# First norm's shift and scale as rows by TensorE, directly behind x's transposes, with the mLSTM constants made between products

## The chip, the cores and the metric

The kernel runs on one core of a Trainium2 chip. The metric is device time in microseconds: the median of three timed runs of the kernel before is 1879.92 us (1876.63 to 1886.28). One further execution was recorded by the hardware profiler.

## The reference, cut to what matters

The program is one layer of a hybrid block: a modulated norm, a projection, an mLSTM mixer beside dilated attention, and an expert-choice feed-forward part. The change touches the first step and a few constants.

```python
mod = silu(c) @ w_ada + b_ada                 # c: 1 x 1024, w_ada: 1024 x 6144
shift1, scale1, gate1, shift2, scale2, gate2 = split(mod, 6)
h = rms_norm(x, norm1_g) * (1 + scale1) + shift1   # x: 1024 x 1024
proj = h @ w_in                                    # 1024 x 2576
```

Of the mLSTM only this matters here: q and k come from the same 4x4 block-diagonal maps, so the kernel forms, for each of four heads, one 128x128 matrix amat (q's map times k's map) and bdv (v's map) from w_q_blk, w_k_blk and w_v_blk.

## The kernel before, in words

`phase_start` does all of the first stage. x comes as eight tiles of 128 tokens (0.52 MB each) by SP's DMA queue. ACT squares each and sums it up (L216), DVE forms the reciprocal roots by a Newton iteration of eleven small operations for four tiles at a time (L134 to L139) and scales the tiles (L244). PE transposes them in two groups of 32 (g = 0 and 1, L248), and ACT and DVE copy the results into xT, which holds k, the 128-wide pieces of the model dimension, in the partitions (L250, L252).

Shift and scale of the norm must stand in the partitions too, one column for each k. `ada_load(k)` fetches w_ada's columns of one k in four DMAs with runs of 512 bytes (L205). For k = 0, PE multiplies them with silu(c) in 16 one-column products (L235). For the others DVE sums eight pieces, each scaled by silu(c) (`ada_sum`, L319 and L321), and PE adds up the partitions by a product with ones (L269). `modulate(k)` then adds the bias and the norm's gain on DVE (L272, L273), POOL applies shift and scale to xT (L274), and `split` makes hTh (fp32r, ACT, L124) and the rest hTl (DVE, L125).

The products of this stage (`mm3_stat`, L332, L334, L336) take three of the four 128-wide chunks of the first 512 columns of w_in, for k = 0 to 7: wh hTh, wh hTl and wl hTh, each for two halves of the tokens, 18 products of 128x512 for a k. The fourth chunk follows for all k, 48 products. So there are 192 products, and behind them the gate projection `gates_proj` begins with the tile wg_h (L332 again). Weights are fetched, copied and split by `w_pair` (L345 on ACT, L346 on DVE or POOL); attention's tables make three small products (L675).

Ahead of it, `consts` has ACT issue ten small DMAs: w_q_blk, w_k_blk and w_v_blk (L155) and seven vectors into the rows of vrows (L170), which PE transposes into vcols (L178, `consts2`). `mlstm_consts` makes masks on POOL, block-diagonal tiles bd on DVE (L442), transposes them on PE (L446, copied at L448), and multiplies them (L451). Both stand in the program between the squares and the roots.

Each engine takes its instructions in the order of the program, apart from small shifts that the build makes; PSUM tiles come from two pools of four (pa and pb), so an order can also wait for a buffer.

Of the kernel before, what the change touches and what calls it, by code (L numbers as in the profile page):

```python
# [16 lines left out]
OP = mybir.AluOpType  # L17
# [93 lines left out]
class K:  # L111
# [30 lines left out]
    def consts(self):  # L142
# [10 lines left out]
        for q, name in enumerate(("w_q_blk", "w_k_blk", "w_v_blk")):  # L153
            src = I[name]
            nc.scalar.dma_start(out=self.w4[:, q], in_=bass.AP(tensor=src.tensor, offset=src.offset, ap=[[4, P], [4 * P, MH], [1, 4]]))  # L155
# [12 lines left out]
        for name, n in (("b_ada", 48), ("norm1_g", 8), ("conv_w", 20), ("conv_b", 4), ("mlstm_norm_g", 4), ("mlstm_skip", 4), ("norm2_g", 8)):  # L168
            src = I[name]
            nc.scalar.dma_start(out=rows[at:at + n, :], in_=bass.AP(tensor=src.tensor, offset=src.offset, ap=[[P, n], [1, P]]))  # L170
# [15 lines left out]
    def phase_start(self):  # L186
# [5 lines left out]
        wada = I["w_ada"].rearrange("(p k) (j n) -> p k j n", k=KT, j=6)  # L192
        with ExitStack() as st:
# [4 lines left out]
            aws, his, los = [], [], []  # L198

            def ada_load(k):  # L200
                aw = [xp.tile([P, KT // 2, 2, P], F32, name="ada_w", **(dict(tag="x", bufs=NT) if 2 <= k < 6 else dict(bufs=4)))
                      for _ in range(2)]
                for h, t in enumerate(aw):
                    for j in range(2):
                        nc.sync.dma_start(out=t[:, :, j, :], in_=wada[:, h * KT // 2:(h + 1) * KT // 2, j, P * k:P * (k + 1)])  # L205
                aws.append(aw)
# [4 lines left out]
            ada_load(0)  # L211
            ada_load(1)
# [5 lines left out]
            self.mlstm_consts()  # L218
            self.consts2()
            accs, pcs = [], []  # L220

            def w_next():
                hi, lo = self.w_pair(0, 512, len(his) // 2, nc.gpsimd if len(his) // 2 % 2 else nc.vector)
                his.extend(hi)
                los.extend(lo)

            def ada_acc(k):

                pcs.append(None)
                if k == 0:  # L230
                    accs.append(None)
                    pcs[k] = self.psB.tile([P, 512], F32, name="pb")
                    for j in range(2):
                        for q in range(KT):
                            nc.tensor.matmul(pcs[k][:, j:j + 1], aws[k][q // 4][:, q % 4, j, :], self.sc[:, q:q + 1], start=(q == 0), stop=(q == KT - 1))  # L235
                else:
# [4 lines left out]
            for g in range(2):  # L241
# [14 lines left out]
                else:  # L256
                    ada_acc(1)
                    for k in range(2, KT):
                        ada_load(k)
# [1462 lines left out]
```

## Time and profile before

| | us |
|---|---|
| median of three timed runs | 1879.92 |
| profiled execution, its own time | 1884.02 |
| its span in the trace | 1882.3 |
| first product of the stage starts | 41.68 |
| first product of the gate projection starts | 100.19 |

Times in a timeline count from the span's start. A matmul's end is modelled, so a row's length has a tail beyond the start of the next one; the pace of a run is read from the starts. An fp32 product shows as two matmul records (two passes), a transpose or an fp32r product as one. Granted clock is the share of TensorE's full speed, 1.00 or 0.50.

### The profile page before, as it was taken

The numbers are of one execution on the slowest core, as the hardware profiler recorded it, in microseconds if no ns is written. First come the engines' busy times: TensorE is split into PE (matmuls) and PEld (weight loads), VectorE is DVE, ScalarE is ACT, GpSimd is POOL, SyncE is SP. The second block draws the span as 40 slices with busy tenths as digits, with TensorE's granted clock in tenths as the row PEclk, the third lists the DMA queues.
The fourth block names the chain that finished last, engine by engine and source line by source line (L and its number), as shares of the span: only waits on it lengthen the run. The fifth ranks groups of instructions, "written<-read, shape, count | busy, mean of one in ns | idle before, by whom it ended". The sixth has DMA issues, their size and how long they took to land. (4 is left out here: it accounts for less than half of the span.)

```text
span 1882.3 us, 23755 instructions
## 1 busy us (share of the span) xinstructions
PE 1774.4 (94%) x8457; PEld 1380.5 (73%) x8457; DVE 1406.9 (75%) x2146; ACT 1119.4 (59%) x1549; POOL 182.6 (10%) x176
## 2 busy tenths in 40 slices
PE   6899999989998939999999999999999999999997
PEld 5677888778886827777777777777777777777775
DVE  5868885687865777777777887777876777867765
ACT  4346454367763537576676666655765766666554
POOL 1301000031123010000100100100100001000000
PEclk9999999999998959999999999999999999999999
DMA  7444663324557777999999999999999989999991
GB/s 234 112 124 141 212 215 110 103 80 117 136 126 210 270 297 291 350 361 356 381 345 367 385 340 368 354 350 359 354 348 351 370 339 376 343 347 344 333 364 34
DMA packets 164492, 517.36 MB, mean 275 GB/s; under 512 B 34614, under 2 KB 68790, under 8 KB 126742
## 3 DMA queue, kind: packets, MB, share of 16 engines
q1 hardware_dynamic: 149376, 482.07, 69.9%
q0 software_dynamic: 10208, 33.10, 7.0%
q8 instruction: 66, 1.08, 0.2%
q10 hardware_dynamic: 4790, 0.68, 0.2%
q14 instruction: 52, 0.43, 0.1%
HBM read 488.29 MB, written 27.50 MB: 274 GB/s over the span
## 5 line engine op out<-in xcount | busy, mean ns | idle before, releaser
L1482 DVE TENSOR_TENSOR wl<-w,wh 128x2048 fp32r<-128x2048 f32 x260 | 585.3, 2280 | 93.1 <-ACT wh L1481 92.5
L1481 ACT ACTIVATE wh<-w 128x2048 fp32r<-128x2048 f32 x260 | 492.3, 1913 | 180.9 <-PE py L1502 80.7
L1481 ACT ACTIVATE wh<-w_half 128x1024 fp32r<-128x1024 f32 x152 | 154.1, 1058 | 68.9 <-PE py L1502 34.9
L1482 DVE TENSOR_TENSOR wl<-w_half,wh 128x1024 fp32r<-128x1024 f32 x152 | 179.0, 1221 | 12.0 <-ACT wh L1481 11.8
L1502 PE MATMUL px<-wh,xTh 128*128 128x512 f32 x448 | 131.4, 411 | 2.1 <-ACT xTh L124 1.6
L1502 PE MATMUL py<-wh,xTh 128*128 128x512 f32 x448 | 131.3, 410 | 1.4 <-ACT wh L1481 1.2
L1502 PE MATMUL py<-wl,xTh 128*128 128x512 f32 x448 | 125.7, 400 | 5.6 <-DVE wl L1482 5.4
L1502 PE MATMUL px<-wl,xTh 128*128 128x512 f32 x448 | 126.3, 402 | 4.4 <-DVE wl L1482 4.4
L1502 PE MATMUL px<-wh,xTl 128*128 128x512 f32 x448 | 124.0, 397 | 0.0
L1502 PE MATMUL py<-wh,xTl 128*128 128x512 f32 x448 | 123.4, 395 | 0.0
L1502 PE MATMUL px<-wh,hT 128*128 128x512 f32 x448 | 118.1, 405 | 0.0
L1502 PE MATMUL py<-wh,hT 128*128 128x512 f32 x448 | 118.1, 405 | 0.0
L1561 POOL DMA_INDIRECT out_dram<-xin,idx x16 | 43.4, 2710 | 673.9 <-DVE xin L1560 673.9
L1502 PEld LDWEIGHTS px<-wl,xTh 128*128 128x128 f32 x448 | 83.6, 189 | 29.3 <-DVE wl L1482 9.5
L1502 PEld LDWEIGHTS py<-wl,xTh 128*128 128x128 f32 x448 | 82.6, 188 | 30.0 <-DVE wl L1482 11.2
L1502 PEld LDWEIGHTS px<-wh,xTh 128*128 128x128 f32 x448 | 83.3, 190 | 28.1 <-issue 6.7
L1502 PEld LDWEIGHTS py<-wh,xTh 128*128 128x128 f32 x448 | 82.9, 188 | 27.1 <-issue 7.7
L1502 PEld LDWEIGHTS px<-wh,hT 128*128 128x128 f32 x448 | 83.2, 188 | 22.8 <-issue 3.8
L1502 PEld LDWEIGHTS py<-wh,hT 128*128 128x128 f32 x448 | 83.0, 188 | 22.8 <-issue 3.8
L1502 PEld LDWEIGHTS px<-wh,xTl 128*128 128x128 f32 x448 | 84.8, 189 | 19.3
L1502 PEld LDWEIGHTS py<-wh,xTl 128*128 128x128 f32 x448 | 84.1, 188 | 19.2 <-DVE xTl L125 0.2
L388 PE MATMUL pa<-wh,hTh 128*128 128x512 f32 x192 | 80.1, 418 | 1.3 <-ACT wh L345 1.2
(458 smaller groups left out, 3371.0 us busy)
## 6 DMA issues: line engine op xcount, KB each, us to landing
w<-in_w_gate_dram SPq DMA_DIRECT2D x100, 1024.0 KB
w<-in_w_up_dram SPq DMA_DIRECT2D x96, 1024.0 KB
w<-in_w_down_dram SPq DMA_DIRECT2D x96, 1024.0 KB
w_half<-in_w_down_dram SPq DMA_DIRECT2D x62, 512.0 KB
w_half<-in_w_up_dram SPq DMA_DIRECT2D x58, 512.0 KB
w_half<-in_w_gate_dram SPq DMA_DIRECT2D x54, 512.0 KB
ada_w<-in_w_ada_dram SPq DMA_DIRECT2D x96, 256.0 KB
wraw<-in_w_in_dram SPq DMA_DIRECT2D x20, 512.0 KB
```

Of the source, the lines that this page charges most:

```text
L388: nc.tensor.matmul(ps, hTh[:, k, t], hi[k], start=(k == 0), stop=False)
L1481: self.nc.scalar.activation(h[:, c], t, AF.Copy)
L1482: self.tc.keep_in_program_order(self.nc.vector.tensor_sub(l[:, c], t, h[:, c]))
L1502: nc.tensor.matmul(ps[c], x[:, t], y[o // m][:, o % m:o % m + 512], start=first and q == 0 and t == 0, stop=last and (q, t) == (len(prods) ...
L1561: nc.gpsimd.indirect_dma_start(out=self.out, out_offset=bass.IndirectOffsetOnAxis(ap=u["idx"][:, :1], axis=0), in_=y, in_offset=None, comp ...
```

## The change

Shift and scale are made for four k at a time (`ada_half(b)`). silu(c) is repeated into 32 columns (screp). For one row of 512 values (shift or scale of four k) PE runs eight products of 32x512, whose outputs stand in four groups of 32 partitions side by side, two products adding up in each. ACT (shift) or DVE (scale) copies the result into SBUF, and four one-column products with sel, which picks one partition of each of the four groups, add the groups up and turn the row into columns. w_ada is fetched in runs of 2048 bytes. `modulate` runs on DVE. Half 0 stands behind all 64 transposes, half 1 behind the products of k = 1. `mlstm_consts` becomes a generator that is advanced between the products of the k's; its masks and `consts2` come after the transposes in the program. All weight splits are on DVE, and the first two weight tiles are fetched earlier. The ten small DMAs are issued by POOL instead of ACT.

```diff
@@ consts @@
-            nc.scalar.dma_start(out=self.w4[:, q], in_=...)
+            nc.gpsimd.dma_start(out=self.w4[:, q], in_=...)
...
-            nc.scalar.dma_start(out=rows[at:at + n, :], in_=...)
+            nc.gpsimd.dma_start(out=rows[at:at + n, :], in_=...)
@@ phase_start @@
+            def ada_load(n, ts):
+                ada[n] = [t.rearrange("p (a n) -> p a n", a=2) for t in ts]
+                for q, t in enumerate(ada[n]):
+                    nc.sync.dma_start(out=t, in_=wada[:, 2 * q:2 * q + 2, n * 512:(n + 1) * 512])
...
-            ada_load(0)
-            ada_load(1)
+            was_x = lambda: [xp.tile([P, D], F32, name="ada_w2", tag="x", bufs=NT) for q in range(4)]
+            own = lambda: [xp.tile([P, D], F32, name="ada_w", bufs=4) for q in range(4)]
+            ada_load(0, own())
+            raws[0] = self.w_raw(0, 512, 0)
...
-            self.mlstm_consts()
-            self.consts2()
+            screp = xp.tile([P, KT, 32], F32, name="silu_c32")
+            nc.vector.tensor_copy(screp, self.sc[:, :, None].to_broadcast([P, KT, 32]))
+            sel = xp.tile([P, 1], F32, name="sel")
+            nc.vector.tensor_reduce(sel, self.ident[:, 0:P:32], axis=AX.X, op=OP.add)
...
                 if g == 0:
-                    ada_acc(0)
-                    w_next()
-                else:
-                    ada_acc(1)
-                    for k in range(2, KT):
-                        ada_load(k)
+                    ada_load(2, was_x())
+                    raws[1] = self.w_raw(0, 512, 1)
+            self.consts2()
+            w_next()
+            consts = self.mlstm_consts()
+            next(consts)
+            def ada_half(b):
+                pc = self.psB.tile([P, 2, 4], F32, name="pb")
+                for j in range(2):
+                    ws = ada[2 * j + b]
+                    ps = self.psB.tile([P, 512], F32, name="pb")
+                    for k in range(KT):
+                        g = slice(32 * (k % 4), 32 * (k % 4) + 32)
+                        nc.tensor.matmul(ps[g, :], screp[:, k, :], ws[k // 2][:, k % 2, :], start=(k < 4), stop=(k >= 4))
+                    row = ws[0][:, 0, :]
+                    if j:
+                        nc.vector.tensor_copy(row, ps)
+                    else:
+                        nc.scalar.activation(row, ps, AF.Copy)
+                    for q in range(4):
+                        nc.tensor.matmul(pc[:, j, q:q + 1], row[:, q * P:(q + 1) * P], sel, start=True, stop=True)
+                mod = xp.tile([P, 2, 4], F32, name="mod", bufs=2)
...
+            def modulate(k):
+                mod = mods[k // 4]
+                nc.vector.tensor_scalar(xT[:, k, :], xT[:, k, :], mod[:, 1, k % 4:k % 4 + 1], mod[:, 0, k % 4:k % 4 + 1], op0=OP.mult, op1=OP.add)
+                self.split(self.hTh[:, k, :], self.hTl[:, k, :], xT[:, k, :])
+            side = itertools.chain(consts, self.attn_tables())
+            ada_half(0)
+            ada_load(1, own())
+            ada_load(3, was_x())
+            for k in range(2):
+                modulate(k)
+            w_next()
+            pss = [[self.xps(t) for b in range(2)] for t in range(3)]
             for k in range(KT):
+                if k % 2 == 0 and k >= 2 and k + 2 < KT:
                     w_next()
                 for c in range(3):
                     self.mm3_stat(pss[c], his[k][:, c * P:(c + 1) * P], los[k][:, c * P:(c + 1) * P], k)
-                if k >= 2:
-                    next(tables, 0)
+                if k == 1:
+                    ada_half(1)
+                if k + 2 < KT:
+                    modulate(k + 2)
+                next(side, 0)
+                if k >= 4:
+                    next(side, 0)
@@ mlstm_consts @@
         for h in range(MH):
+            yield
```

The first place is PE from its start to the first products (L332 before, L338 now; vrows the vector rows, bd and bdT mLSTM constants). Before:

```order
L178 MATMUL pa<-ident,vrows 128x128
L446 MATMUL pb<-ident,bd 128x128 x2
L451 MATMUL pb<-bdT_177,bdT_171 128x128
...
L248 MATMUL pb<-ident,x 128x128 x32
L235 MATMUL pb<-silu_c,ada_w 128x1 x16
L248 MATMUL pb<-ident,x 128x128 x32
L269 MATMUL pb<-ones,ada_acc 128x1 x2
L332 MATMUL pa<-hTh,wh 128x512 x4
```

Now, on the same engine and stretch:

```order
L235 MATMUL pb<-ident,x 128x128 x16
L178 MATMUL pa<-ident,vrows 128x128
L235 MATMUL pb<-ident,x 128x128 x48
L257 MATMUL pb<-ada_w,silu_c_149 32x512 x8
L264 MATMUL pb<-sel,ada_w 128x1 x4
L257 MATMUL pb<-ada_w_219,silu_c_149 32x512 x2
...
L264 MATMUL pb<-sel,ada_w_219 128x1 x4
L338 MATMUL pa<-hTh,wh 128x512 x4
```

The transposes come first, the transpose of vrows stands after 16 of them, and two rows with their column products stand ahead of the first product of the stage.

The second place is PE between the products of the first k's. Before, behind most of the products of k = 1:

```order
L332 MATMUL pb<-hTh,wh 128x512 x2
L334 MATMUL pb<-hTl,wh 128x512
L269 MATMUL pb<-ones,ada_acc 128x1 x2
L334 MATMUL pb<-hTl,wh 128x512
L336 MATMUL pb<-hTh,wl 128x512 x2
L269 MATMUL pb<-ones,ada_acc 128x1 x2
```

Now, at the same place and a little on:

```order
L342 MATMUL pb<-hTh,wl 128x512 x2
L257 MATMUL pb<-ada_w,silu_c_149 32x512 x8
L338 MATMUL pa<-hTh,wh 128x512 x2
L340 MATMUL pa<-hTl,wh 128x512 x2
L264 MATMUL pb<-sel,ada_w 128x1 x4
L257 MATMUL pb<-ada_w_359,silu_c_149 32x512 x2
```

Half 1 took the place of the pairs of L269, of which there was one for each k. Four products of k = 2 stand between its first row and that row's column products.

The third place is POOL's start: ident is the identity that all transposes use, bmask the mask of the mLSTM constants. Before:

```order
masks.py:197 MEMSET ident 128x128
L422 MEMSET mask 128x256
masks.py:199 ISA
masks.py:199 AFFINE_SELECT ident<-ident 128x128
L423 AFFINE_SELECT mask<-mask 128x128
```

Now:

```order
masks.py:197 MEMSET ident 128x128
L155 DMA w_80<-in_w_q_blk_dram 128x4x4
masks.py:199 ISA
masks.py:199 AFFINE_SELECT ident<-ident 128x128
L155 DMA w_80<-in_w_k_blk_dram 128x4x4
L155 DMA w_80<-in_w_v_blk_dram 128x4x4
L170 DMA vrows<-in_b_ada_dram 48x128
```

The ten DMAs, of which six more rows follow here, stand ahead of every mask, one of them between the two steps that make ident.

## Rows read from the trace of the kernel before

**Rows 1.** The page, first part: busy time and share of the span, PE first.
```profile
PE 1774.4 (94%) x8457; PEld 1380.5 (73%) x8457; DVE 1406.9 (75%) x2146; ACT 1119.4 (59%) x1549; POOL 182.6 (10%) x176
```

**Rows 2.** Stretches: length, each engine's busy us, clock, DMA share, GB/s.
```profile
0.00:9.00 9.00, 0.00 (x0) 0.00 (x0) 0.30 (x2) 1.26 (x1) 2.69 (x13) 1.00 0.81 230
...
9.00:16.00 7.00, 2.47 (x8) 1.48 (x8) 3.04 (x15) 6.99 (x15) 0.00 (x0) 1.00 1.00 354
...
16.00:26.00 10.00, 7.01 (x24) 4.77 (x25) 7.80 (x35) 3.74 (x10) 0.00 (x0) 1.00 1.04 287
...
32.60:39.30 6.70, 6.70 (x33) 6.70 (x33) 4.56 (x10) 2.30 (x4) 1.20 (x1) 0.50 0.79 230
...
41.68:100.19 58.51, 52.20 (x222) 38.46 (x223) 46.87 (x96) 18.75 (x20) 19.14 (x20) 1.00 0.47 129
```

**Rows 3.** Waits until 100 us: waiter <- releaser: total us, times, longest.
```profile
ACT hTh L124 <- POOL xT L274: 19.6, 6, 6.8
...
ACT L213 <- DMA vrows<-in_conv_w_dram: 7.7, 1, 7.7
...
PE pa L332 <- ACT hTh L124: 4.8, 4, 1.9
...
PE pa L334 <- DVE hTl L125: 2.6, 4, 1.2
```

**Rows 4.** Timeline to 42 us: start, length, engine, line, operation, count, idle before.
```profile
9.14 1.04 ACT L216 ACTIVATE xT<-x 128x1024 f32<-128x1024 f32 x1
...
20.98 2.74 DVE L244 TENSOR_SCALAR x<-x,rs 128x1024 f32<-128x1024 f32 x4
...
23.64 0.16 DVE L134 TENSOR_SCALAR n_v<-ss 128x4 f32<-128x4 f32 x1
...
23.78 5.98 PE L248 MATMUL pb<-ident,x 128*128 128x128 f32 x29 [0.19 <-DVE x L244]
...
25.82 2.74 DVE L244 TENSOR_SCALAR x<-x,rs 128x1024 f32<-128x1024 f32 x4
...
33.59 6.51 PE L248 MATMUL pb<-ident,x 128*128 128x128 f32 x32
...
40.58 1.05 ACT L124 ACTIVATE hTh<-xT 128x1024 fp32r<-128x1024 f32 x1
...
41.68 1.20 PE L332 MATMUL pa<-hTh,wh 128*128 128x512 f32 x4 [1.24 <-ACT hTh L124]
```

**Rows 5.** Timeline of PE where the gate projection begins.
```profile
99.74 0.61 PE L336 MATMUL pb<-hTh,wl 128*128 128x512 f32 x2
100.19 0.62 PE L332 MATMUL pa<-hTh,wg_h 128*128 128x512 f32 x2
```

**Rows 6.** Timeline, prices of single kinds: ACT copy, column products, small DVE, fp32 passes.
```profile
24.36 0.60 ACT L252 ACTIVATE xT<-pb 128x512 f32<-128x512 f32 x1 [3.50 <-DMA mk<-in_c_mask_dram]
...
29.60 4.13 PE L235 MATMUL pb<-silu_c,ada_w 128*128 128x1 f32 x32
...
51.38 0.23 DVE L272 TENSOR_TENSOR mod<-pb,vcols 128x1 f32<-128x1 f32 x2 [0.36 <-PE pb L269]
...
157.40 1.98 PE L543 MATMUL pb<-xc,amat 128*128 128x512 f32 x4
...
159.22 0.60 PE L553 MATMUL pb<-ident,xc 128*128 128x128 f32 x4
...
159.65 1.06 PE L561 MATMUL pb<-bdv,xm 128*128 128x128 f32 x8
...
441.57 1.09 PE L863 MATMUL op<-pT,vs 128*64 128x128 f32 x16
```

**Rows 7.** Groups until 100 us: busy, mean ns: the second half of a split.
```profile
L125 DVE TENSOR_TENSOR hTl<-xT,hTh 128x1024 fp32r<-128x1024 f32 x8 | 9.7, 1218 | 3.3 <-ACT hTh L124 3.2
```

**Rows 8.** Timeline of POOL: a DMA that it issues itself.
```profile
143.22 0.77 POOL L509 DMA_DIRECT2D gate_rows_d<-row_W  x1 [1.62 <-ACT row_W L505]
```

**Rows 9.** Line 1561: durations in ns, least, median and most.
```profile
L1561 POOL DMA_INDIRECT out_dram<-xin,idx x16: 1552/3381/3402, 822.6 to 1872.0; - x16
```

More of the change, by code (lines that the diff above doesn't have):

```diff
@@ L169, in consts @@
             src = I[name]
-            nc.scalar.dma_start(out=rows[at:at + n, :], in_=bass.AP(tensor=src.tensor, offset=src.offset, ap=[[P, n], [1, P]]))
+            nc.gpsimd.dma_start(out=rows[at:at + n, :], in_=bass.AP(tensor=src.tensor, offset=src.offset, ap=[[P, n], [1, P]]))
             self.vec_rows[name] = at
@@ L253, in phase_start @@
                 if g == 0:
-                    ada_acc(0)
-                    w_next()
-                else:
-                    ada_acc(1)
-                    for k in range(2, KT):
-                        ada_load(k)
-            tables = self.attn_tables()
-            pss = None
-            def modulate(k):
-                pc = pcs[k]
-                if pc is None:
-                    pc = self.psB.tile([P, 512], F32, name="pb")
-                    for j in range(2):
-                        nc.tensor.matmul(pc[:, j:j + 1], accs[k][:, j, :], self.ones[:, 0:1], start=True, stop=True)
-                mod = xp.tile([P, 2], F32, name="mod", bufs=2)
-                for j in range(2):
-                    nc.vector.tensor_add(mod[:, j:j + 1], pc[:, j:j + 1], self.vcol("b_ada", 8 * j + k))
-                nc.vector.scalar_tensor_tensor(mod[:, 1:2], mod[:, 1:2], 1.0, self.vcol("norm1_g", k), op0=OP.add, op1=OP.mult)
-                nc.gpsimd.tensor_scalar(xT[:, k, :], xT[:, k, :], mod[:, 1:2], mod[:, 0:1], op0=OP.mult, op1=OP.add)
-                self.split(self.hTh[:, k, :], self.hTl[:, k, :], xT[:, k, :])
@@ L277, in phase_start @@
-            modulate(0)
-            for k in range(KT):
-                if k and k + 1 < KT:
-                    ada_acc(k + 1)
-                if k + 1 < KT:
-                    modulate(k + 1)
-                if k % 2 == 0 and k + 2 < KT:
-                    w_next()
-                if pss is None:
-                    pss = [[self.xps(t) for b in range(2)] for t in range(3)]
+                    ada_load(2, was_x())
+                    raws[1] = self.w_raw(0, 512, 1)
+            self.consts2()
@@ new lines, in phase_start @@
+            w_next()
+            consts = self.mlstm_consts()
+            next(consts)
+            mods = []
+            def ada_half(b):
[14 more added lines that the diff above has]
+                mod = xp.tile([P, 2, 4], F32, name="mod", bufs=2)
+                for j in range(2):
+                    nc.vector.tensor_add(mod[:, j], pc[:, j], self.vcol("b_ada", 8 * j + 4 * b, 4))
+                nc.vector.scalar_tensor_tensor(mod[:, 1], mod[:, 1], 1.0, self.vcol("norm1_g", 4 * b, 4), op0=OP.add, op1=OP.mult)
+                mods.append(mod)
@@ L292, in phase_start @@
+            for _ in side:
                 pass
```

48 lines of the change are left out of this document (17 added, 31 removed).

## The prediction

> **What bounds the kernel now.** I read the page's first part, then the table of stretches, the list of waits of the first 100 us, and the timelines of PE, DVE, ACT and POOL there. Over the whole execution PE is busy 94% [rows 1], and from the gate projection (its first product at 100.19 us, [rows 5]) on, the order of instructions is the same in both kernels on all five engines. So what the change does to the time is what it does to that moment; everything later should move with it. The profiled execution took 1884.02 us (span 1882.3); the median of the three timed runs is 1879.92. I work out a difference from the profiled execution and apply it to the median.
>
> The 100.19 us have two parts. Until 41.68 us PE waits for the front: x must land, be squared, scaled and transposed, and one k be modulated [rows 4]. Between 41.68 and 100.19 PE is the bound with holes: 192 products at 0.226 us (two start 0.45 us apart, [rows 5]) are 43.4 us of 58.5 [rows 2]; 7.4 us are waits for hTh and hTl [rows 3], and hTh in turn waited 19.6 us for POOL's modulation; the rest are three table products, six pairs of column products of L269 and shorter holes.
>
> **The front, part by part.** (1) *ACT's queue.* Ten DMA issues leave ACT, whose first activation waited 7.7 us behind them [rows 3]. ACT then squares each x as it lands. Until 9 us 230 GB/s arrive, 2.07 MB, about four tiles of 0.52 MB; until 16 us another 354 GB/s [rows 2], which carries the eighth to some 15.3 us. The fourth is squared (1.04 us and the accumulator's read, [rows 4]) at 10.4.
> (2) *DVE.* Before, the reciprocal roots stood among the mLSTM constants and the first x was scaled at 20.98 [rows 4]. Now the eleven small operations come at once (23.64 to 25.82, 2.2 us, [rows 4]) and four scalings of 0.69 (2.74 for four): all four x's at 15.3. The second four: squared at 16.7; six mask products moved ahead of the roots cost 1.5 us inside this gap (estimate: 0.25 each, an eighth of the 1.22 of 128x1024 with two inputs, [rows 7], and 0.1); roots 2.2, the copy of vcols 0.3 (an estimate like the 0.25), scaling 2.7: 22.0 to 23, I take 22.
> (3) *Transposes.* 32 of them took 6.51 us at a granted clock of 0.50 ([rows 2], [rows 4]); four elsewhere at 1.00 took 0.60 with a tail of 0.27, 0.11 each [rows 6]. The ones of 23.78 to 29.76 went at 0.206 each, the slow pace, although the table of stretches has 1.00 for the start of the execution, so I take the clock as low at the start. The first 32 then run 15.3 to 22.0. The clock was 0.50 for 6.7 us filled by transposes alone and 1.00 from 41.68 on [rows 2], so it rises on transposes, and I expect it up during the first 32 or early in the second; the second 32 are then held by their copies (0.60 on ACT and about as much on DVE in turn, 0.45 us for a group of four): 3.6 us at the fast end, 6.6 at the slow one. I take 5: 27.0.
> (4) *The rows by TensorE.* One row is 8 products of 32x512, fp32 in two passes each: 16 passes. A pass of 512 columns is 0.43 us (four in 1.98 with a tail of 0.6, [rows 6]), so 6.9 us one behind the other. Side by side: L863 has two column groups, and its 16 passes of 128 columns took 1.09 us, while 8 passes alone took 1.06 [rows 6]: two groups are free of each other. Four groups are not shown. Bounds 1.7 (all four) and 6.9 (none); I take 1.9, nearest to what L863 does. By the Trainium skill (TensorE: Matmul & The Clock Gate, Part 3) three column groups gave 2.38 times, so four would give some 3.2: 2.2 us a row, an estimate, and the sum 1.2 us worse.
> After each row: copy 0.60 and 0.2 until it starts; eight passes of one column at 0.129 (32 in 4.13, [rows 6]), 1.0. Row one: 27.0 + 1.9 + 0.8 + 1.0 = 30.7. Row two needs its weights. Bytes: x 4.19, own weights 2.10, first w_in 0.52, then 2.10 into x's tiles, free at 22.0; with 0.3 MB of small ones 9.2 MB. 4.55 are in by 16 us; 4.65 at 287 GB/s [rows 2] take 16.2: 32.2. So row two ends near 32.8 by its weights, not by PE, and PE's pace in (3) matters little. Then copy 0.9, column products 1.0, 0.36 of wait and 0.6 for three small DVE operations (0.23 for the first two, [rows 6]), modulate on DVE 0.75 (the form of the scaling of x), hTh 1.05 [rows 4] and 0.2: **first product at 37.6 instead of 41.68, 4.1 us earlier.**
> (5) *POOL.* Its ten DMAs are software-issued. One cost 0.77 us [rows 8], an indirect one up to 3.4 [rows 9]. I take 0.8: the last leaves at 9, the masks are done at 12, both before PE's vrows transpose (at 18.6, in the middle of the first 32) and DVE's mask products (15.3) ask. They are hidden by x's way; above some 1.6 us each they are not (a rival).
>
> **From the first product to the gates.** Added on PE: half 1 of the rows, 2 x 1.9 and 2 x 1.0, 5.8; eight constant transposes and four products of two passes, 8 x 0.2 + 8 x 0.13, 2.6, which before lay in the idle front. Removed: the L269 pairs (24 passes here, some 3.1) and most of the waits, since DVE needs 0.75 + 1.22 for a k and half of 1.22 for weights ([rows 7]), 2.6 of the 4.1 us that PE needs, and hTh no longer waits for POOL. I keep 0.9 for the first hTl, behind two modulations and one weight split on DVE, and 1.5 for the rest. 43.4 + three table products 2.6 + 5.8 + 2.6 + 2.4 = 56.8 against 58.5: 1.7 earlier. Half 1's weights (0.52 MB of w_in, then 4.2 MB, from 32 us on at 287 GB/s) land near 41 for its first row and 49 for its second; PE, two k's in, asks for them at about 47 and 51.
>
> Sum: 4.1 + 1.7 = **5.8 us earlier, 1878.2 in the profiled execution, 1874 of the median.** That is 0.31%. A measurement of this kernel can tell about 0.5%, 9.4 us, from no change, so the likeliest verdict is the same time. Even if every bound falls well (second 32 in 3.6, weights at 354 GB/s, no hole), the first product comes at some 35.5 and the gates' at 91: 9 us.
>
> **Rivals.**
> *The clock falls before the products.* Between 32.8 and 37.6 PE has only one-column products. In the kernel before, the stretch with 32 of those (29.60 to 33.73, [rows 6]) was followed by a granted clock of 0.50 until 39.3 [rows 2]. Fallen at 37.6, it stretches 3.4 us of products to 6.8. For it: the hole of 4.8 us. Against: the dense rows on either side. Result 1877.5. The Trainium skill (TensorE: Matmul & The Clock Gate, Part 4) says that transposes do not count as PE activity. By that the clock would stay at 1.2 GHz through both 32s and the rows, and cost the transposes 1.6 and the rows 3.4 us more, 1879. This trace disagrees: the clock rose with transposes alone ahead of it [rows 2].
> *The column groups do not run together.* 6.9 instead of 1.9 for four rows is 20 us, of which 1.9 lie under the second row's weights: 1879.9 - 5.8 + 18 = 1892, slower. It decides from some 3.7 us a row on, where the gain is gone. Against it is L863 [rows 6]. Two at a time, 3.4 us a row: +4.1, 1878.
> *POOL's DMAs are late.* At 2.7 us each the last vector lands at 30; PE's queue holds the vrows transpose after 16 of the 64, and all behind it waits: 48 transposes 5.6 to 9, then rows, and the first product at 48: +10, 1884.5. For it: POOL's indirect DMA [rows 9]. The Trainium skill (SBUF — State Buffer, SBUF: two separate sides) adds that VectorE in a two-port mode keeps GpSimd from writing descriptors, which speaks against moving DMAs to POOL. No row here shows it for a DMA. DVE has no long operation before 12.5 us.
> *It only changes places.* What the front gains, PE pays back with 8.4 us of added products, if waits stay at the 7.4 of before: 1880.
>
> **How the numbers follow.** Forecast 0.52 (its own range 1869 to 1879); clock 0.15; changed places or two at a time 0.13; POOL 0.07; one after another 0.05; everything falls well 0.08 (1871). Faster by over 0.5% (under 1870.5): half of the last case and a sixth of the forecast, whose own spread and the measurement's reach that far, 0.14. Slower (over 1889.3): the column rival and a fifth of POOL's, 0.06. The same: 0.80. The range 1867 to 1885 leaves out the column rival, half of POOL's and the ends.
>
> **What would show it.** Right: ACT's first square before 6 us; x scaled near 12 to 15; the four rows' 64 passes with starts in bunches of four, 1.7 to 2.2 us a row; the last w_ada of the second row landing about when PE asks; first product at 35 to 39; gates' first product at 92 to 97; no POOL modulation. Wrong: a vrows transpose that waits for a DMA of POOL's queue, rows of over 3 us, granted clock 0.50 under products, or waits for hTh and hTl that add up to more than 4 us again. If the gates start 5 us earlier and the end does not, the later part is not rigid as assumed.

## The result, and the profile after

| | before | after |
|---|---|---|
| median of the runs beside it | 1880.66 us (4 runs) | 1868.78 us (4 runs, 1868.47 to 1869.41) |
| ratio of the times, 95% interval | | 0.9937 [0.9918, 0.9955] |
| profiled execution, its own time / span | 1884.02 / 1882.3 | 1869.41 / 1867.7 |
| first product of the stage | 41.68 | 36.59 |
| first product of the gate projection | 100.19 | 93.72 |

The change gained. It gained 6.5 us until the gate projection, where 5.8 were predicted, and more behind it, where nothing was predicted. A second comparison of the same two kernels (e1 below) gave 0.9958 [0.9944, 0.9973]. Over all runs of this study the mean of before is 1880.9 us (80 runs, standard deviation 3.4), that of after 1870.3 (11 runs, 1.8). The chips differ: before's means lie between 1880.0 and 1883.0. Against the runs of before beside it, after's mean is 12.2 us less in the first comparison and 8.9 in the second, which has more runs.

The page's first part, against [rows 1]; PE works 7 us less in all:

```profile
PE 1767.7 (95%) x8493; PEld 1369.8 (73%) x8493; DVE 1382.7 (74%) x2086; ACT 1121.6 (60%) x1551; POOL 170.2 (9%) x176
```

The front, by the timeline of the changed kernel to 42 us (columns as in [rows 4]):

```profile
4.51 1.04 ACT L222 ACTIVATE xT<-x 128x1024 f32<-128x1024 f32 x1
...
10.26 0.51 POOL L170 DMA_DIRECT2D vrows<-in_norm_g_dram  x1 [1.24 <-DMA w<-in_w_k_blk_dram]
...
13.89 2.74 DVE L231 TENSOR_SCALAR x<-x,rs 128x1024 f32<-128x1024 f32 x4
...
14.79 3.86 PE L235 MATMUL pb<-ident,x 128*128 128x128 f32 x16 [14.79 <-DVE x L231]
...
20.87 2.74 DVE L231 TENSOR_SCALAR x<-x,rs 128x1024 f32<-128x1024 f32 x4
...
26.64 1.92 PE L257 MATMUL pb<-ada_w,silu_c 128*32 128x512 f32 x16
...
28.66 0.60 ACT L262 ACTIVATE ada_w<-pb 128x512 f32<-128x512 f32 x1 [1.13 <-PE pb L257]
...
29.30 1.05 PE L264 MATMUL pb<-sel,ada_w 128*128 128x1 f32 x8 [0.74 <-ACT ada_w L262]
...
30.29 1.92 PE L257 MATMUL pb<-ada_w,silu_c 128*32 128x512 f32 x16
...
36.59 2.08 PE L338 MATMUL pa<-hTh,wh 128*128 128x512 f32 x4 [2.52 <-ACT hTh L124]
```

Against [rows 4], ACT squares from 4.51 instead of 9.14, the first four x's are scaled from 13.89 instead of 20.98, and the second four from 20.87, which is 5 us earlier than before. A row by TensorE takes 1.92 us, its tail included, and the second row starts straight behind the column products, with no wait for weights. The row of four products at 36.59 is 2.08 us long, tail included, where before's was 1.20: their starts are 0.43 us apart from the second on instead of 0.23, half pace. The stretches of the changed kernel (columns as in [rows 2]) show the clock for it:

```profile
9.00:16.00 7.00, 1.21 (x6) 1.05 (x6) 4.24 (x15) 5.21 (x11) 2.50 (x9) 1.00 1.03 380
...
26.00:36.59 10.59, 6.52 (x55) 3.24 (x53) 5.48 (x10) 4.29 (x7) 0.00 (x0) 0.91 1.04 382
36.59:41.48 4.89, 4.89 (x13) 3.81 (x14) 4.83 (x8) 1.96 (x2) 0.00 (x0) 0.50 1.04 389
41.48:93.71 52.23, 52.23 (x251) 38.12 (x250) 27.16 (x48) 17.79 (x23) 2.19 (x11) 1.00 0.23 63
```

The first 4.89 us of the products ran at 0.50 (1.2 GHz), which costs 2.4 us (half of it); behind them PE is busy in 52.23 of 52.23 us, where [rows 2] had 52.20 of 58.51. The waits until 94 us (waiter <- releaser: total us, times, longest; answer to [rows 3]) say the same:

```profile
ACT hTh L124 <- DVE xT L274: 12.0, 3, 5.6
...
PE pa L338 <- ACT hTh L124: 2.5, 1, 2.5
...
POOL vrows L170 <- DMA w<-in_w_q_blk_dram: 1.6, 1, 1.6
```

PE waits for hTh once, ahead of the first product; hTh no longer waits for POOL, and its waits for DVE cost PE nothing.

Behind the gates the two profiled executions differ by the clock. Stretches of before at 0.50 behind the gates:

```profile
141.78:148.60 6.82, 5.93 (x20) 4.82 (x21) 6.60 (x11) 5.17 (x5) 2.01 (x4) 0.50 0.09 13
199.81:206.63 6.82, 5.87 (x14) 4.67 (x15) 6.22 (x13) 5.92 (x14) 0.00 (x0) 0.50 0.76 227
394.37:397.78 3.41, 3.41 (x18) 3.41 (x17) 2.43 (x10) 3.40 (x13) 0.47 (x1) 0.50 0.00 0
585.51:595.75 10.24, 8.53 (x25) 7.18 (x26) 7.49 (x9) 2.52 (x4) 5.25 (x7) 0.50 0.98 271
660.60:701.56 40.96, 9.78 (x36) 7.41 (x37) 32.34 (x148) 12.37 (x17) 6.50 (x11) 0.50 0.74 289
```

And of after:

```profile
137.06:140.47 3.41, 3.41 (x9) 2.65 (x9) 3.28 (x7) 3.06 (x3) 1.12 (x3) 0.50 0.03 5
191.67:195.08 3.41, 3.41 (x10) 2.63 (x9) 1.86 (x3) 2.83 (x4) 0.00 (x0) 0.50 0.79 243
567.14:570.55 3.41, 3.41 (x10) 2.64 (x9) 0.51 (x1) 1.55 (x3) 0.87 (x1) 0.50 1.17 223
645.64:686.60 40.96, 9.83 (x36) 7.46 (x37) 32.14 (x146) 12.42 (x17) 6.45 (x11) 0.50 0.74 291
```

Without the long one at the routing, which both have, and one at the very end (8.6 us before, 8.9 after, not shown), before spent 27.3 us at half speed behind the gates and after 10.2. Half of the difference is 8.5 us; what came on top of the gates' 6.5 in this pair of traces is 8.1 (spans 14.6 apart). So the clock accounts for it by its size, if a stretch at 0.50 costs half its length. Whether the change brings it was the question of the experiments.

### The profile page after: what moved, and what is told of

The parts are those of the page before. It is cut to its first block, busy times and chain, and to the rows that moved or that the text cites. A ratio compares the mean times of both kernels' runs of the same rounds, so it can differ in the third digit from the quotient of the medians.

```text
span 1867.7 us, 23741 instructions
## 1 busy us (share of the span) xinstructions
PE 1767.7 (95%) x8493; PEld 1369.8 (73%) x8493; DVE 1382.7 (74%) x2086; ACT 1121.6 (60%) x1551; POOL 170.2 (9%) x176
## 5 line engine op out<-in xcount | busy, mean ns | idle before, releaser
L1514 PEld LDWEIGHTS py<-wl,xTh 128*128 128x128 f32 x448 | 82.6, 188 | 30.0 <-DVE wl L1494 11.3
```

The lines of the kernel that those rows point to most:

```text
L1514: nc.tensor.matmul(ps[c], x[:, t], y[o // m][:, o % m:o % m + 512], start=first and q == 0 and t == 0, stop=last and (q, t) == (len(prods) ...
```

## The experiments

Ratios are to runs of before on the same chip, beside them.

**e1: the changed kernel again, nothing altered.**

> The changed kernel once more, unaltered, for the spread of its own times and for a second trace. In the two profiled executions the gates' first product comes 6.5 us earlier after the change, and the end 14.9 us earlier; 8.5 us of that is the difference in half-speed clock after the gates (27.3 us at 0.50 before, 10.2 after, half of which is lost). Theory A (the fall of the clock belongs to the kernel: the holes lie in the same place against the clock's steps in every execution): the median is 1868.8 again within 0.7, all runs within 1.5 us, and the new trace has the same three falls after the gates with the same lengths. Theory B (it is drawn anew in every execution): the new trace has other lengths of half speed after the gates, and the runs spread by 3 to 10 us as those of before do (1876.6 to 1886.3).

Measured: 1871.59 us median (7 runs, 1869.09 to 1874.00), ratio 0.9958 [0.9944, 0.9973]. Its trace has the gates at 93.52 and the same stretches at 0.50 as the first one, plus one of 3.42 us at 580.62. (The ends of the first two traces lie 14.6 us apart, not the 14.9 of the expectation.) In this pair of traces theory A holds for three falls and B for one. In the times B holds: they spread over 4.9 us, and the median is 2.8 above that of the first four runs, which lay within 1 us of each other.

**e2: the changed kernel, started later.**

```diff
+            for i in range(5):
+                nc.sync.dma_start(out=xT[:, i, :], in_=I["x"][i * P:(i + 1) * P, :])
             for i in range(NT):
                 nc.sync.dma_start(out=xs[i], in_=I["x"][i * P:(i + 1) * P, :])
```

> The changed kernel with five loads of 0.52 MB ahead of x on SP's queue (into xT, which is overwritten): all of it starts later by some 6.5 to 6.9 us (five tiles at 380 GB/s), so that the gates start where they do in the kernel before, near 100.4 us. Theory A1 (the later gain of 8.5 us belongs to where the holes lie against the clock's steps, counted from the program's start): the half-speed stretches of the kernel before come back, 27 us after the gates, and the time is 1868.8 + 6.7 + up to 8.5, 1879 to 1884. Theory A2 (the later gain belongs to what the change leaves behind in queues and buffers, whatever the time it starts): 1875.5 with the falls of the changed kernel. Theory B (drawn anew in every execution): 1875 to 1884 with a spread of over 3 us between runs.

Measured: 1878.95 (12 runs, 1875.56 to 1884.66), 0.9999 [0.9987, 1.0011]. The gates started at 99.39, 5.7 us later than in the changed kernel, 0.8 earlier than before; the mean is 0.7 under before's. Its stretches at 0.50 behind the gates are others than either kernel's (6.8 us at 141.90, 3.4 at 387.66, 3.4 at 486.64, 6.8 at 582.22). So A2 falls: the code behind the change does not by itself gain anything late. A1 falls too in its strict form, since before's stretches do not come back. B's times and spread fit, and its reason, a draw in every execution, is what is left; whether the moment of the holes counts as well, these runs do not tell.

**e3: only the DMAs on POOL and the constants between products, shift and scale as before.**

```diff
-            nc.scalar.dma_start(out=self.w4[:, q], in_=...)
+            nc.gpsimd.dma_start(out=self.w4[:, q], in_=...)
...
-            nc.scalar.dma_start(out=rows[at:at + n, :], in_=...)
+            nc.gpsimd.dma_start(out=rows[at:at + n, :], in_=...)
...
-            self.mlstm_consts()
-            self.consts2()
...
+            self.consts2()
+            consts = self.mlstm_consts()
+            next(consts)
+            tables = itertools.chain(consts, self.attn_tables())
```

> The kernel before with two parts of the change alone: the ten small DMAs issued by POOL, and the vector transpose and the mLSTM constants behind x's transposes, the constants between products. Shift and scale are made for each k as before (DVE sums, one-column products, POOL's modulation). My working: the roots then come right behind the squares, x is scaled by some 15 instead of 23.7 us, the transposes end near 27 to 28 instead of 40, but k = 0's shift and scale and POOL's modulation stay, and the stretch to the gates keeps its waits for POOL and gets the constants' products (2.6 us). First product near 33 to 36, stretch to the gates 60 to 62, gates at 94 to 97: 1874 to 1878 if the rest moves with it. Rival (the rows by TensorE are what gains, and the order alone gains nothing because DVE's sums for k = 1 to 7 are then the bound): first product not before 40, gates at 99 to 102, 1880.

Measured: 1885.20 (12 runs), 1.0033 [1.0016, 1.0051]. Both theories missed a half: the first product came early, the gates did not. PE's timeline, then waits of POOL and ACT, then stretches:

```profile
34.19 1.65 PE L334 MATMUL pa<-hTh,wh 128*128 128x512 f32 x3 [6.05 <-ACT hTh L124]
...
100.36 0.61 PE L334 MATMUL pa<-hTh,wg_h 128*128 128x512 f32 x2
```

```profile
POOL xT L275 <- DVE mod L274: 49.9, 8, 18.7
ACT hTh L124 <- POOL xT L275: 31.2, 7, 7.8
```

```profile
34.20:49.85 15.65, 13.23 (x56) 10.68 (x56) 14.68 (x36) 2.51 (x4) 3.65 (x2) 0.83 0.97 264
49.85:60.09 10.24, 8.88 (x25) 6.30 (x25) 9.33 (x21) 3.28 (x5) 5.68 (x3) 0.50 0.21 58
```

7.5 us won at the first product, all of it lost by the gates: hTh waited 31.2 us for POOL's modulation (19.6 before, [rows 3]), DVE was busy in 24.0 of the 25.9 us of the two stretches, and PE's pauses were followed by 10.24 us at 0.50. POOL in turn waited 49.9 us for DVE's shift and scale (18.7 of them ahead of the first), so the reason that the rival gave, DVE's sums, holds for this part. The time is worse than both theories said (1874 to 1878, and 1880).

**e4: only the rows by TensorE, with the DMAs and the constants where they were.**

```diff
-            nc.gpsimd.dma_start(out=self.w4[:, q], in_=...)
+            nc.scalar.dma_start(out=self.w4[:, q], in_=...)
...
-            nc.gpsimd.dma_start(out=rows[at:at + n, :], in_=...)
+            nc.scalar.dma_start(out=rows[at:at + n, :], in_=...)
...
+            self.mlstm_consts()
+            self.consts2()
             screp = xp.tile([P, KT, 32], F32, name="silu_c32")
...
-            self.consts2()
             w_next()
-            consts = self.mlstm_consts()
-            next(consts)
```

> The changed kernel with the other half undone: the ten small DMAs back on ACT, and the vector transpose and the mLSTM constants made ahead of the roots as before; the rows by TensorE, the wide loads of w_ada, DVE's modulation and the weight tiles stay. My working: the first x is scaled at 21 as before, the transposes end near 36 to 38, rows, copies, columns and modulation add 10 us, so the first product comes at 46 to 48; the stretch to the gates is 2.6 us shorter than 57.1 and has no half-speed part: 52 to 54; gates at 99 to 101: 1876 to 1880, no gain. Rival (most of the gain comes from the rows and DVE's modulation): gates at 95 or earlier, 1870 to 1874.

Measured: 1881.55 (12 runs), 1.0012 [1.0000, 1.0024]; gates at 100.60. PE's timeline:

```profile
32.98 1.92 PE L256 MATMUL pb<-ada_w,silu_c 128*32 128x512 f32 x16
...
44.77 1.65 PE L336 MATMUL pa<-hTh,wh 128*128 128x512 f32 x3 [2.52 <-ACT hTh L124]
```

As expected in the gates (99 to 101 were said); the time is 1.5 us above the range expected. The rows stand 12 us ahead of the first product and make the front longer, unless the transposes end early. Each half of the change alone gains nothing (gates +0.2 and +0.4 us); together they gain 6.5. So the order frees the front's time, and the rows with DVE's modulation, which end the waits for POOL, keep it.

**e5: a row's products one behind the other.**

```diff
-                        g = slice(32 * (k % 4), 32 * (k % 4) + 32)
-                        nc.tensor.matmul(ps[g, :], ..., start=(k < 4), stop=(k >= 4))
+                        nc.tensor.matmul(ps[:32, :], ..., start=(k == 0), stop=(k == KT - 1))
...
```

In the part left out the copies and the column products take 32 partitions instead of 128.

> The changed kernel with the eight products of a row accumulating in one group of 32 partitions, one behind the other, instead of in four groups side by side; the column products then contract over 32 partitions. Nothing else is altered. Theory (the four groups of 32 columns run at the same time, 16 passes in 1.92 us): a row's 16 passes come one by one at 0.43 us and take 6.9 us, 5.0 more for each of four rows; the first product of the stage comes at 46 to 47 instead of 36.6, the gates' at 112 to 115 instead of 93.7, and the time is some 20 us more than the changed kernel's, 1889 to 1893, 9 to 13 more than before. Rival (the products are quick because they have 32 columns of weights, not because the groups run together): a row stays under 3 us and the time moves by less than 5 us.

Measured: 1891.73 (4 runs), 1.0077 [1.0056, 1.0099]; gates at 114.22. PE's timeline:

```profile
26.00 7.05 PE L256 MATMUL pb<-ada_w,silu_c 128*32 128x512 f32 x16
33.73 1.05 PE L263 MATMUL pb<-ident,ada_w 32*128 32x1 f32 x8 [0.68 <-ACT ada_w L261]
34.71 7.05 PE L256 MATMUL pb<-ada_w,silu_c 128*32 128x512 f32 x16
```

16 passes take 7.05 us in one group of columns and 1.92 in four. The theory holds to the microsecond; this is what the prediction's heaviest rival would have cost. The rows keep their 32 columns of weights, so few columns alone are not what makes them quick.

**e6: the front tightened.** A half's two rows directly one behind the other, mask products and the copy of vcols kept behind the scalings, and 11 products of ident by ident before the first product of the stage.

```diff
...
+            ps = self.psB.tile([P, 512], F32, name="pb")
+            for i in range(11):
+                self.tc.keep_in_program_order(nc.tensor.matmul(ps[:, :P], self.ident, self.ident, ...))
...
```

> The changed kernel with its front tightened: a half's two rows by TensorE directly one behind the other (the first row's copy then lies under the second row's products), the mLSTM mask products and the copy of vcols kept out of DVE's way until the roots and scalings are through, and 11 products of ident by ident (into a PSUM tile that nothing reads) between the last column product and the first product of the stage, so that PE does not stand still there. Theory: the second row starts when its last weights are in, near 29.5, the first product comes at 34.5 to 35.5 instead of 36.6, and the clock is 1.00 from there on instead of 0.50 until 41.5 (2.5 us): gates' first product at 89.5 to 91 instead of 93.7, and about 3 us less than the changed kernel's median. Rival (mask products and the copies that now stand between hTl and modulation cost what the front gains): gates' first product at 92 to 94, no change. Rival for the clock (it falls all the same): products at half pace behind 35.

Measured: 1867.79 (6 runs), 0.9937 [0.9921, 0.9954]. Stretches of its trace:

```profile
0.00:34.40 34.40, 18.31 (x136) 13.79 (x136) 17.25 (x47) 20.59 (x35) 8.80 (x23) 1.00 0.97 343
34.40:89.47 55.07, 54.90 (x264) 40.18 (x263) 32.89 (x61) 19.76 (x25) 2.19 (x11) 1.00 0.32 100
```

First product at 34.40, gates at 89.47, clock 1.00 throughout: the theory holds as far as the gates. From first product to gates 55.07 instead of 57.1 us, with 264 matmul records on PE against 262, so the half-speed start cost 2.0 us. The gates come 4.2 us earlier than after's; of that the mean of the times shows 2.4 against all runs of after, where some 3 were expected.

**e7: the ten DMAs back on ACT alone** (the two `nc.gpsimd.dma_start` of `consts` as `nc.scalar.dma_start`).

> The changed kernel with the ten small DMAs back on ACT and nothing else undone by hand. The build then puts the transpose of vrows at the very start of PE's queue, and the copy of vcols and six mask products ahead of DVE's first roots. Theory: ACT's first square comes at 9.1 instead of 4.5, the fourth at 14 instead of 11.4, and the first x is scaled near 16.6 instead of 13.9; but the eighth is squared at 19.2 instead of 16.9, its roots then need no pause, and the second four are scaled within 1 us of where they are now (20.9). Rows, first product and gates move by 0 to 1.5 us: the DMAs on POOL are worth little by themselves. Rival (they are what frees the front): first product later by 3 us or more, gates at 96.5 or later, 1872 to 1875.

Measured: 1873.08 (8 runs), 0.9966 [0.9952, 0.9979]; gates at 94.33, 0.6 later than after. ACT and DVE in its timeline:

```profile
8.88 1.04 ACT L222 ACTIVATE xT<-x 128x1024 f32<-128x1024 f32 x1
...
15.38 2.74 DVE L231 TENSOR_SCALAR x<-x,rs 128x1024 f32<-128x1024 f32 x4
...
20.21 2.74 DVE L231 TENSOR_SCALAR x<-x,rs 128x1024 f32<-128x1024 f32 x4
```

The first four x's are scaled 1.5 us later (2.7 were expected), the second four 0.7 earlier. By the gates, the DMAs on POOL are worth under a microsecond.

**e8: PE's holes behind the gates filled**, ahead of the gate rows' transposes, of the routing's prefix products and of the experts' first transposes.

```diff
+                for i in range(16 if j == 1 else 0):
+                    nc.tensor.matmul(ps[:, 3 * P:], b_[:, :P], b_[:, :P], start=True, stop=True)
...
+        for i in range(44):
+            self.tc.keep_in_program_order(nc.tensor.matmul(ps[:, 3 * P:], self.ident, self.ident, start=True, stop=True))
...
+            for i in range(16):
+                self.tc.keep_in_program_order(nc.tensor.matmul(ps[:, 3 * P:], self.ident, self.ident, start=True, stop=True))
```

> The changed kernel with idle PE time filled at three places behind the gate projection, by products whose results nobody reads: 16 ahead of the transposes of the gate rows (the hole of 4.0 us at 132), 44 ahead of the routing's prefix products (the hole of 14.7 us at 652) and 16 ahead of the first transposes of the experts' tokens (the hole of 5.4 at 672). Theory (the time behind the gates differs between executions by the half-speed stretches that follow such holes): no clock of 0.50 follows the hole at 136 (3.4 to 6.8 us at half speed in the traces, so 1.7 to 3.4 us gained), the clock is back at 1.00 well before 677 instead of at 686.6 (up to 4.5 us gained): 1863 to 1868, and the runs spread less. Rival (the clock falls by something else than idle PE, or the added products themselves hold up what waits behind them): the half-speed stretches stay or the products run past the ends of the holes, and the time is the same or up to 5 us more.

Measured: 1873.88 (11 runs), 0.9961 [0.9947, 0.9974]: no gain over after (its mean is 2.9 us longer). The first filling, whose operand row_h comes late, made PE stand still with work behind it. Its timeline and stretches:

```profile
130.71 7.19 PE L525 MATMUL pb<-row_h 36*128 36x128 f32 x32 [2.77 <-DVE row_h L495]
```

```profile
130.48:144.14 13.66, 13.43 (x52) 11.62 (x53) 11.27 (x15) 7.29 (x7) 4.55 (x8) 0.50 0.10 25
...
662.96:673.20 10.24, 8.19 (x73) 8.00 (x72) 9.77 (x62) 0.00 (x0) 1.56 (x3) 1.00 0.84 351
673.20:683.44 10.24, 5.87 (x32) 5.39 (x33) 7.76 (x14) 0.00 (x0) 3.10 (x5) 0.50 0.10 25
```

A wait of 2.77 us, and 13.66 us at half speed, although PE was busy in nearly all of them. At the routing the filling brought the clock back at 662.96, and pauses of 3.2, 1.9 and 1.3 us behind it were followed by 0.50 again. By PE's starts against after's trace, the first place lost 3.7 us and the routing gained 3.0 (2.4 against e1's trace). The rival holds for the one, the theory for the other.

**e9: e6 and the routing filled more densely** (56, 6 and 20 products, nothing at the gate rows).

> The tightened front of e6 and, as the only filling behind the gates, products of ident by ident whose results nobody reads around the routing: 56 ahead of the prefix products (hole of 14.7 us), 6 ahead of the transposes of the ranks (1.9) and 20 ahead of the first transposes of the experts' tokens (5.4); no filling in the gate rows' hole, where it made PE wait in e8. Theory (what idle PE time costs behind it is the half-speed stretch that follows): the 41 us of 0.50 around the routing end about 10 us in, the first products of the experts run at full pace, and 3.5 to 4.5 us go: median 1863 to 1865 against e6's 1867.8. Rival (gaps of 1 to 3 us that are left let the clock fall again, as at 673 in e8): 2 us or less, 1866 or more.

Measured: 1866.51 (6 runs), 0.9923 [0.9907, 0.9939]. Around the routing 13.65 and 3.41 us at 0.50 were left instead of 40.96, but the last one fell on the experts' first products (681.46 to 684.87, behind a pause of 2.0). By PE's starts the routing gained 2 us, so the size is the rival's.

**e10 and e11: one multiplication from POOL to DVE, in before and in after.** In the traces, one place near 389 us (379 after) goes in two ways. Before, POOL and DVE, then PE:

```profile
388.86 2.36 POOL L747 TENSOR_TENSOR qk<-qk,gqk 128x1024 f32<-128x1024 f32 x1 [17.09 <-PE sp L806]
...
389.03 2.74 DVE L416 TENSOR_TENSOR og<-og,ev 128x512 f32<-128x512 f32 x1 [0.49 <-ACT ev L414]
...
394.07 0.36 PE L805 MATMUL sp<-kTh,qT 128*128 128x256 f32 x1 [4.06 <-DVE stats L812]
```

After, the same instructions:

```profile
378.70 0.69 DVE L427 TENSOR_TENSOR og<-og,ev 128x512 f32<-128x512 f32 x1 [0.23 <-ACT ev L425]
...
378.79 2.86 POOL L759 TENSOR_TENSOR qk<-qk,gqk 128x1024 f32<-128x1024 f32 x1 [17.34 <-ACT ev L425]
...
380.14 0.39 PE L817 MATMUL sp<-kTh,qT 128*128 128x256 f32 x1 [1.88 <-ACT ev L425]
...
383.08 0.36 PE L817 MATMUL sp<-kTh,qT 128*128 128x256 f32 x1 [1.24 <-DVE stats L824]
```

Which of the two starts first, by 0.1 to 0.2 us, decides whether DVE's product takes 0.69 or 2.74 us. With it goes, in these two, whether PE has one hole of 4.06 or two of 1.88 and 1.24.

```diff
-        nc.gpsimd.tensor_mul(y, y, self.gqk[...])
+        (nc.vector if hp == 1 else nc.gpsimd).tensor_mul(y, y, self.gqk[...])
```

> The kernel before with one multiplication moved from POOL to DVE: the gain of q for the second attention pair (qk times gqk, near 389 us), nothing else; the order of all other instructions is the same. In the traces so far it and DVE's og product start within 0.2 us of each other; where POOL's is first, DVE's takes 2.7 to 2.9 instead of 0.69, PE stands still 3.4 to 4.1 us and a stretch at 0.50 follows (before, e3, e4, e7); where DVE's is first, PE has two holes of 1.9 and 1.2 and mostly no such stretch (changed kernel, e1, e5, e6, e8). Theory R (this start decides a systematic part of the 3.3 us by which the changed kernel gains more on average, 9.9, than its gates do, 6.6): before gets 1.4 us from the hole and up to 1.7 to 3.4 from the clock, mean 1876 to 1878.5 instead of 1880.1, and the changed kernel with the same edit (e11) gains under 1, so that the two differ by 6 to 8. Theory D (the 3.3 are draws of the clock elsewhere): before moves by under 1 and the two still differ by 9 to 11.

> The changed kernel with the same one multiplication moved from POOL to DVE. Theory R: the og products take 0.69 each, the holes near 378 and 382 become shorter by some 0.4 us in all, no stretch at 0.50 there as before, mean 1869 to 1870.5 (1870.3 over eleven runs of the changed kernel), and 6 to 8 us under e10. Theory D: mean 1869 to 1871 too, but 9 to 11 us under e10.

The list in the first of these has e3 in the wrong place. There DVE's product came first (388.20, 0.69 us), and still PE had a hole of 3.35 and 6.8 us at 0.50. Of all fourteen traces, POOL's is first in four (before, e4, e7, e9), with a hole of 3.5 to 4.1 us and a stretch at 0.50 in each; DVE's is first in seven, with such a stretch in two (e2, e3).

Measured: before with the edit 1877.98 (12 runs, mean 1877.9), 0.9977 [0.9962, 0.9992]; after with it 1870.80 (6 runs, mean 1871.4, 1867.12 to 1877.29), 0.9949 [0.9928, 0.9969]. DVE and PE in the trace of before with the edit, then the stretch behind the hole:

```profile
390.44 0.68 DVE L416 TENSOR_TENSOR og<-og,ev 128x512 f32<-128x512 f32 x1
...
393.43 0.36 PE L805 MATMUL sp<-kTh,qT 128*128 128x256 f32 x1 [2.93 <-DVE stats L812]
...
393.73:397.14 3.41, 3.41 (x18) 3.41 (x17) 2.43 (x10) 3.40 (x13) 0.48 (x1) 0.50 0.01 3
```

DVE's product takes 0.68 again and PE's hole is 2.93 (2.90 in e11). The stretch at 0.50 is still there, 3.41 us as in before (394.37), so this trace shows theory R's 1.1 us of the hole and not its gain by the clock. Before gained 3.0 us in the mean against all its runs, 4.1 against those beside it; after gained nothing. The two differ by 6.5, 95% interval about 3 to 10, which is theory R's size; theory D's 9 to 11 is not excluded. It leans to R by the times alone and is not settled.

**e12: e9 with that multiplication on DVE.**

> e9 (tightened front, routing filled) with the multiplication of e10 and e11 on DVE as well. In e9's trace POOL's multiplication came first near 376, PE stood still 4.04 us and a stretch of 3.4 us at 0.50 followed. Theory R: the hole falls to 2.9 us as in e10 and e11, PE goes on 1.1 us earlier: the mean falls by 1 to 3 from e9's 1866.4, to 1863.5 to 1865.5, ratio to before near 0.991. Theory D (no systematic part there): within 1 us of e9.

Measured: 1865.51 (6 runs, mean 1865.5), 0.9909 [0.9893, 0.9925]. It is 0.9 under e9 in the mean, 1.9 when each is taken against the runs of before beside it, so this too leans to R without deciding. In its trace the hole is 2.77 and 3.41 us at 0.50 still follow (378.77). It beats both kernels: 17 us under the runs of before beside it and, by the means, 4.8 under after.

## Why the prediction was right as far as the gates, and short behind them

**The front.** First product at 36.59, predicted 37.6. The steps came in the order said, some with errors that cancel. The fourth x was squared at 11.3 (predicted 10.4), so the first four x's were scaled by 16.6 (15.3) and the second four by 23.6 (22.0). But PE began with the first x, at 14.79 (15.3), and the second 32 transposes took 4.9 us (5), so all were over at 26.64 (27.0). A row took 1.92 (1.9), copy and column products what they were priced at. The term that was off is the second row's weights: I had PE held by them until 32.2; they came at 382 GB/s (stretch 26.00 to 36.59 above) where I took 287 [rows 2], and PE did not wait for them: row two ended near 32.2 instead of 32.8.

**Between first product and gates.** 57.1 us, predicted 56.8, by two errors that cancel. I kept 2.4 us of stalls, and there were none. And the first rival came true: the clock fell in the hole of 2.5 us ahead of the products, which cost 2.4 (e6: 2.0), where the rival said 3.4. It had a chance of 0.15, so that the sum comes out here is luck.

**Column groups.** All four run together, 1.92 us. e5 shows the other end: 7.05 a row and 1892, what the rival said. The Trainium skill (TensorE: Matmul & The Clock Gate, Part 3) has 2.38 times for three groups; here four give 7.05 / 1.92 = 3.7 times, so the trace is above its scaled figure. On transposes (the Trainium skill, TensorE: Matmul & The Clock Gate, Part 4) the trace disagrees a second time: the granted clock rose at 21.0 us (starts 0.21 us apart until there, 0.11 behind), when PE had done nothing but transposes. The prediction's own row for it is not as clean as it says: of the stretch of 32.60 to 39.30 the first us was column products, and transposes alone stand ahead of the rise from 33.59 on.

**POOL's DMAs.** 0.5 to 1.0 us each, the last one left at 10.77 (predicted 9) since two waited for earlier ones to land (1.6 and 1.2). PE's transpose of vrows did not wait. That rival did not happen.

**The step that failed** is the first paragraph's "everything later should move with it". The order of the instructions behind the gates is the same, the times are not. In the pair of traces the later part gained another 8.1 us, in the means 5.7 and 2.2 (table below). Before's own gates are not fixed either: e10's kernel is the same up to there and has them at 101.09, 0.9 later (four traces of after's front agree within 0.2), so up to 0.9 of this may belong ahead of the gates. So the medians are 1868.8 and 1871.6 instead of 1874. They lie in the stated range because the range was wide, not because the sum held behind the gates. The chance of 0.14 stood for a gain of over 0.5%; the ratios are 0.63% and 0.42%, so whether it was too small is open. Against that assumption stood the spread of before's three runs, 10 us wide, which I read as measurement only. It is in the main how the time behind the gates differs from one execution to the next. The Trainium skill (TensorE: Matmul & The Clock Gate, Part 1) says that what governs the clock runs freely, so that the same kernel meets it differently from run to run; the fall at 580.62 that one of two traces of the same kernel has agrees. The clearest rows are those of the hole of 4.0 us ahead of the gate rows' transposes, which all traces but e8's have: 3.4 us at 0.50 follow in eight of them and 6.8 in five, and both with the same code up to there (6.8 in before, 3.4 in e10; 6.8 in e6 and e9, 3.4 in e12).

Shift of the gates in each trace, mean shift of the runs against before's beside them, and what is left for the later part:

| kernel | gates | runs | later part |
|---|---|---|---|
| after, first comparison (4 runs) | -6.5 | -12.2 | -5.7 |
| after again, e1 (7) | -6.7 | -8.9 | -2.2 |
| e2, started later (12) | -0.8 | -0.7 | +0.1 |
| e3, order alone (12) | +0.2 | +5.5 | +5.3 |
| e4, rows alone (12) | +0.4 | +1.5 | +1.1 |
| e5, rows serial (4) | +14.0 | +12.9 | -1.1 |
| e6, front tightened (6) | -10.7 | -12.0 | -1.3 |
| e7, DMAs on ACT (8) | -5.9 | -7.5 | -1.6 |

The shifts of 6 to 12 runs have a standard error of 0.8 to 1.4 us, those of 4 runs about 2. So the gates' moment carries most of the time, and the later part adds between -6 and +5 with no rule that these runs give. It goes with the clock: taking half of the stretches at 0.50 (the routing's aside) from the time between gates and end leaves 1766.6 to 1770.1 us in the traces of before, after, e1 to e7, e10 and e11, where the uncorrected times go from 1774.0 to 1782.1. Shown is that holes of PE are followed by such stretches and that their number and lengths differ between executions (after and e1, and the hole of 4.0 us). The same code, started 5.7 us later, has no late gain in the mean (e2). Open is how much of the changed kernel's 2.2 to 5.7 us there is more than a draw, and why: the order of POOL and DVE near 389 is one part that e10's times make likely, at 1 us by its trace and up to 4 by its runs. Why e3 has 5 us more than its trace's gates is open too; one execution was profiled, at 1882.43, under its mean of 1885.6.

## What to carry to other kernels

A forecast that ends at "from here on the order is the same" should still look at the holes of PE behind that point: each may be followed by a stretch at half speed whose length differs from run to run, and the spread of the times shown hints at how much that is worth (here 10 us, as much as the change gained). Two edits that shorten the front and the stage may each gain nothing alone: e3 and e4 together are worth 6.5 us, apart nothing. And small products of 32 columns gained 3.7 times here when their outputs were put side by side in PE's four column groups; the price is four one-column products a row with sel, which add the groups up.

## What the hardware did that was not expected

- A DVE product of 0.69 us took 2.74 when POOL's product of 2.36 us had started 0.17 us ahead of it, and POOL's took 2.86 when DVE was first by 0.09. The Trainium skill (SBUF — State Buffer, SBUF: two separate sides) calls the port pair of VectorE and GpSimd an exclusive lock that whoever starts first keeps for the whole instruction, for VectorE operations with two inputs in SBUF as well; these rows agree. A start that moves by 0.2 us moved PE by 1 us.
- Eleven products of ident by ident, 2.70 us of PE ahead of the first product, and the clock stayed at 1.00 (e6, and e9 and e12 with the same filling), where it fell in the eight other traces that have the rows by TensorE; a pause of 2.77 us that a filling itself caused was followed by 13.66 us at 0.50 with PE busy (e8).
- From 9 to 16 and from 26 to 36.6 us the loads moved 380 and 382 GB/s (321 between, at a DMA share of 0.92); the kernel before had 354 and 287 at 9 and 16 us [rows 2], the 287 at a share of 1.04 as the 382 now. Its runs of w_ada are 512 bytes, now 2048; that this is the cause was not tried.
